# Huber loss over 8192 x 8192 floats: the middle tiles in two pieces of 6624 columns instead of three of 4416

## The chip, the core and the metric

The kernel runs on one NeuronCore of a Trainium2 chip. The metric is device time in microseconds for one execution. The parts that matter are VectorE (DVE in the profile), ScalarE (ACT), the sync engine SP, which here only issues transfers, and the core's 16 DMA engines, which move data between device memory (HBM) and the on-chip memory SBUF with its 128 partitions.

## The reference

```python
def reference(pred, target):          # both 8192 x 8192 float32
    delta = 1.0
    diff = pred - target
    abs_diff = np.abs(diff)
    return np.where(abs_diff <= delta, 0.5 * diff**2, delta * (abs_diff - 0.5 * delta))
```

The output is a float32 array of the same shape. Two arrays of 268.4 MB are read and one is written. There is no reduction: each element is computed alone.

## The kernel before

The kernel uses that the loss equals max(|d| - 0.5, 0.5 clip(d)^2), with d = pred - target and the clip to [-1, 1]. Five instructions make it, in place in two buffers a and b: VectorE subtracts (a = a - b, L82) and clips (b = clip(a), L83); ScalarE squares with a scale (b = 0.5 b^2, L86) and takes the absolute value (a = |a|, L87); VectorE closes with b = max(a - 0.5, b) (L76). b is then stored.

The arrays are seen as flat: 524288 columns for each of 128 partitions. They are cut into n = 40 tiles. Tile 0 and tile 39 are 10432 columns wide; the 38 between them have W = 13248, which is 6624 KB for one array. There are two buffers for a and two for b. Tile i uses buffer i modulo 2, and the output of a tile is stored from its b buffer.

All transfers are issued from SP's queue, in program order: the loads of tiles 0 and 1, and then for each tile i the store of tile i and the loads of tile i + 2. Each instruction of this queue waits for what it needs, and whatever is behind it waits too. The store (L68) waits for the last max of tile i. The load of a for tile i + 2 (L49) goes into the buffer that tile i has just finished with, and follows at once. The load of b for tile i + 2 must wait until the store of tile i has landed, since it overwrites what is being stored.

Middle tiles are loaded in one transfer for a and one for b. Tiles 0 and 1 arrive in halves (`HALVES`, L51). Tile 38 arrives as three quarters of a, half of b, the last quarter of a, the other half of b; tile 39 in six pieces (L55 and L56). The last tile is also stored in pieces: three of two eighths, two of one eighth.

`compute(i)` (L70) cuts a tile into pieces of equal width: 2 for tile 0, 4 for tile 38, 8 for tile 39 (`PARTS`, L58), and 3 for all others (L80), which makes pieces of 4416 columns. For each piece it issues subtract and clip on VectorE and Square and Abs on ScalarE. The max of a piece is not issued at once, since it needs ScalarE's result: pieces wait in the list `todo`, and `finish(keep)` (L73) issues the max of the oldest until only `keep` are left. With `finish(2)` (L89) VectorE is up to two pieces ahead of ScalarE; in a tile of three pieces all subtracts and clips come first, then the three maxes. The order is written out by hand: no scheduler moves anything.

Of the kernel before, what the change touches and what calls it, by code (L numbers as in the profile page):

```python
# [1 line left out]

# [4 lines left out]


@with_exitstack
def kernel(  # L10
    ctx: ExitStack,
    tc: tile.TileContext,
    pred: bass.AP,
    target: bass.AP,
    out: bass.AP,
):
    nc = tc.nc
    P = 128
    fp32 = mybir.dt.float32
    Alu = mybir.AluOpType  # L20
    Act = mybir.ActivationFunctionType
    SQRT_HALF = 0.70710678118654752

    total = pred.shape[0] * pred.shape[1] // P
    W = 13248

    ends = total % W + W
    widths = [ends - ends // 2] + [W] * (total // W - 1) + [ends // 2]
    n = len(widths)
    starts = [sum(widths[:i]) * P for i in range(n)]  # L30

    def block(x, i):
        flat = x.rearrange("r m -> (r m)")
        return flat[starts[i] : starts[i] + P * widths[i]].rearrange("(p m) -> p m", p=P)

    pool = ctx.enter_context(tc.tile_pool(name="slots", bufs=1))
    a_slots = [pool.tile([P, W], fp32, name=f"a{k}") for k in range(2)]
    b_slots = [pool.tile([P, W], fp32, name=f"b{k}") for k in range(2)]

    def shares(i, parts):  # L40
        w = widths[i] // parts
        edges = [k * w for k in range(parts)] + [widths[i]]
        return [slice(edges[k], edges[k + 1]) for k in range(parts)]

    def load(i, which, first, last):
        quarters = shares(i, 4)
        c = slice(quarters[first].start, quarters[last].stop)
        dst, src = (a_slots, pred) if which == "a" else (b_slots, target)
        nc.sync.dma_start(out=dst[i % 2][:, c], in_=block(src, i)[:, c])  # L49

    HALVES = (("a", 0, 1), ("b", 0, 1), ("a", 2, 3), ("b", 2, 3))  # L51
    LOADS = {
        0: HALVES,
        1: HALVES,
        n - 2: (("a", 0, 2), ("b", 0, 1), ("a", 3, 3), ("b", 2, 3)),  # L55
        n - 1: (("a", 0, 2), ("b", 0, 0), ("b", 1, 1), ("b", 2, 2), ("a", 3, 3), ("b", 3, 3)),  # L56
    }
    PARTS = {0: 2, n - 2: 4, n - 1: 8}  # L58

    def store(i):  # L60
        if i == n - 1:
            eighths = shares(i, 8)
            pieces = [slice(eighths[k].start, eighths[k + 1].stop) for k in (0, 2, 4)]
            pieces += eighths[6:]
        else:
            pieces = shares(i, 1)
        for c in pieces:
            nc.sync.dma_start(out=block(out, i)[:, c], in_=b_slots[i % 2][:, c])  # L68

    def compute(i):  # L70
        todo = []

        def finish(keep):  # L73
            while len(todo) > keep:
                a, b = todo.pop(0)
                nc.vector.scalar_tensor_tensor(  # L76
                    out=b, in0=a, scalar=-0.5, in1=b, op0=Alu.add, op1=Alu.max
                )

        for c in shares(i, PARTS.get(i, 3)):  # L80
            a, b = a_slots[i % 2][:, c], b_slots[i % 2][:, c]
            nc.vector.tensor_tensor(out=a, in0=a, in1=b, op=Alu.subtract)  # L82
            nc.vector.tensor_scalar(  # L83
                out=b, in0=a, scalar1=-1.0, scalar2=1.0, op0=Alu.max, op1=Alu.min
            )
            nc.scalar.activation(out=b, in_=b, func=Act.Square, scale=SQRT_HALF)  # L86
            nc.scalar.activation(out=a, in_=a, func=Act.Abs)  # L87
            todo.append((a, b))
            finish(2)  # L89
        finish(0)  # L90

    ctx.enter_context(tc.manual_schedule())

    def load_all(i):
        for piece in LOADS.get(i, (("a", 0, 3), ("b", 0, 3))):
            load(i, *piece)

    load_all(0)
    load_all(1)
    for i in range(n):  # L100
        compute(i)
        store(i)
        if i + 2 < n:
            load_all(i + 2)


# [1 line left out]
_INS = ['pred', 'target']  # L108
_OUTS = [((8192, 8192), 'float32')]


# [23 lines left out]
```

## Time and profile before

| what | value |
|---|---|
| median of 3 runs | 1868.83 us (1868.62 to 1869.63) |
| the profiled execution | 1869.48 us |
| its span, first to last instruction | 1867.7 us |
| VectorE busy | 1405.9 us, 375 instructions |
| ScalarE busy | 903.7 us, 251 instructions |
| read and written | 536.87 MB and 268.44 MB, 431 GB/s over the span |
| VectorE's wait for loads of b | 442.1 us in 41 waits |
| ScalarE's wait for the clip | 949.7 us in 48 waits |
| SP's wait for stores to land | 994.6 us in 38 waits |

The span is what the profiler sees between the first and the last instruction. The page lists busy time by engine, a strip of 40 equal slices of the span with the busy share of each engine and of the DMA engines in tenths, the DMA queues, the chain of work that ended last, the costliest groups of instructions, and the DMA issues with the median time from issue to landing. A group's line reads: source line, engine, operation, output and inputs by tile name, shape, count, busy time in us, mean duration of one in ns, and then the idle time of the engine just before these instructions and what ended it. SPq is SP's queue.

### The profile page before, as it was taken

What the parts mean: (1) busy time and instruction counts of PE and PEld (TensorE: products, weight loads), DVE (VectorE), ACT (ScalarE), POOL (GpSimd) and SP (SyncE); (2) the same over time, 40 slices, a digit from 0 to 9 for tenths busy, and PEclk for the clock granted to TensorE, in tenths of its full rate; (3) what the DMA queues carried; (4) which work ended last, traced back from release to release, by engine and by line L of the source; (5) the groups of instructions that cost most, each with busy time, mean ns of one, the idle gap of its engine ahead of it and who ended that gap; (6) DMA issues with size and microseconds to landing.
All of it is one profiled execution on the core that took longest, in us unless ns stands there. A gap on an engine that the chain in (4) does not pass through costs nothing.

```text
span 1867.7 us, 983 instructions
## 1 busy us (share of the span) xinstructions
DVE 1405.9 (75%) x375; ACT 903.7 (48%) x251; POOL 0.2 (0%) x4
## 2 busy tenths in 40 slices
DVE  4877777777777777777777777777777777777796
ACT  4444444444444444444444444444444444444464
POOL 0000000000000000000000000000000000000000
DMA  9999999999999999999999999999999999999998
GB/s 410 432 429 434 432 436 433 435 433 431 431 436 431 436 434 436 435 431 431 434 434 435 435 435 436 435 429 434 434 431 436 434 435 436 435 429 435 430 428 377
DMA packets 19303, 805.37 MB, mean 431 GB/s; under 512 B 2144, under 2 KB 2144, under 8 KB 2400
## 3 DMA queue, kind: packets, MB, share of 16 engines
q1 hardware_dynamic: 19296, 805.31, 99.8%
q14 instruction: 7, 0.06, 0.0%
HBM read 536.87 MB, written 268.44 MB: 431 GB/s over the span
## 4 chain that ended last, share of the span: by engine, by line
DMA 60%; DVE 38%; issue 1%; ACT 0%; DVEq 0%; another core or an unknown queue 0%; SPq 0%
DMA b<-in_target_dram 32%; DMA out_dram<-b 28%; DVE a L82 15%; DVE b L76 15%; DVE b L83 8%; ACT b L86 0%; ACT a L87 0%; DVEq L130 0%; SPq L49 0%; DVEq L82 0%
## 5 line engine op out<-in xcount | busy, mean ns | idle before, releaser
L86 ACT ACTIVATE b<-b 128x4416 f32<-128x4416 f32 (+3 forms) x125 | 461.0, 3688 | 949.7 <-DVE b L83 949.7
L82 DVE TENSOR_TENSOR a<-a,b 128x4416 f32<-128x4416 f32 (+3 forms) x125 | 565.2, 4522 | 442.1 <-DMA b<-in_target_dram 442.1
L76 DVE SCALAR_TENSOR_TENSOR b<-a,b 128x4416 f32<-128x4416 f32 (+3 forms) x125 | 558.5, 4519 | 3.6 <-ACT a L87 3.6
L87 ACT ACTIVATE a<-a 128x4416 f32<-128x4416 f32 (+3 forms) x125 | 460.3, 3682 | 0.0
L83 DVE TENSOR_SCALAR b<-a 128x4416 f32<-128x4416 f32 (+3 forms) x125 | 293.0, 2344 | 4.3
L86 ACT ACT_TABLE_LOAD x1 | 1.3, 1283 | 0.7 <-PEq L119 0.7
L119 POOL MEMSET const-bfloat16-1.0<- 128x1 bf16 x1 | 0.1, 101 | 0.0
L119 POOL MEMSET const-uint8-127<- 128x1 uint8 x1 | 0.1, 101 | 0.0
L119 POOL MEMSET const-float32-0.0<- 128x1 f32 x1 | 0.1, 98 | 0.2 <-issue 0.2
L119 POOL MEMSET const-float32-1.0<- 128x1 f32 x1 | 0.1, 98 | 0.0
## 6 DMA issues: line engine op xcount, KB each, us to landing
out_dram<-b SPq DMA_DIRECT2D x38, 6624.0 KB, 26.9
a<-in_pred_dram SPq DMA_DIRECT2D x36, 6624.0 KB, 42.1
b<-in_target_dram SPq DMA_DIRECT2D x36, 6624.0 KB, 31.3
b<-in_target_dram SPq DMA_DIRECT2D x4, 3312.0 KB, 35.5
a<-in_pred_dram SPq DMA_DIRECT2D x2, 3312.0 KB, 40.5
a<-in_pred_dram SPq DMA_DIRECT2D x2, 2608.0 KB, 14.5
b<-in_target_dram SPq DMA_DIRECT2D x2, 2608.0 KB, 20.3
out_dram<-b SPq DMA_DIRECT2D x1, 5216.0 KB, 21.3
```

The costliest lines, as they stand in the source:

```text
L76: nc.vector.scalar_tensor_tensor(out=b, in0=a, scalar=-0.5, in1=b, op0=Alu.add, op1=Alu.max)
L82: nc.vector.tensor_tensor(out=a, in0=a, in1=b, op=Alu.subtract)
L83: nc.vector.tensor_scalar(out=b, in0=a, scalar1=-1.0, scalar2=1.0, op0=Alu.max, op1=Alu.min)
L86: nc.scalar.activation(out=b, in_=b, func=Act.Square, scale=SQRT_HALF)
L87: nc.scalar.activation(out=a, in_=a, func=Act.Abs)
L119: nc = _bacc.Bacc("TRN2", target_bir_lowering=False, num_devices=1)
```

## The change

Every tile without an entry in `PARTS` (tiles 1 to 37) is computed in two pieces of 6624 columns instead of three of 4416. The argument of `finish` inside the loop goes from 2 to 1, so that a max is held back by one piece only. This second edit applies to every tile: in tiles 38 and 39, whose pieces stay as they were, the max of piece k now follows the clip of piece k + 1 instead of that of piece k + 2. In tile 0, with two pieces, the order of instructions stays. Loads, stores, buffers and the order of SP's queue are not touched.

```diff
-        for c in shares(i, PARTS.get(i, 3)):
+        for c in shares(i, PARTS.get(i, 2)):
             a, b = a_slots[i % 2][:, c], b_slots[i % 2][:, c]
             nc.vector.tensor_tensor(out=a, in0=a, in1=b, op=Alu.subtract)
             nc.vector.tensor_scalar(
...
             nc.scalar.activation(out=b, in_=b, func=Act.Square, scale=SQRT_HALF)
             nc.scalar.activation(out=a, in_=a, func=Act.Abs)
             todo.append((a, b))
-            finish(2)
+            finish(1)
         finish(0)
```

## The prediction

> **What bounds the kernel now.** I read the page first: engines, the DMA strip, the queues, the chain.
>
> ```profile
> DVE 1405.9 (75%) x375; ACT 903.7 (48%) x251; POOL 0.2 (0%) x4
> ...
> DMA  9999999999999999999999999999999999999998
> ...
> q1 hardware_dynamic: 19296, 805.31, 99.8%
> ...
> DMA 60%; DVE 38%; issue 1%; ACT 0%; DVEq 0%; another core or an unknown queue 0%; SPq 0%
> ```
>
> Two views disagree. The strip and the queue say that the 16 DMA engines are never idle: then only bytes count, and they do not change. The chain says that 38% of the end time is DVE, so longer work on a tile would lengthen the run. What settles it is the order of one ordinary tile. From the timeline (start, duration; SPq lines are issues, idle time in brackets):
>
> ```profile
> 999.41 4.76 DVE L82 TENSOR_TENSOR a<-a,b 128x4416 f32<-128x4416 f32 x1 [11.41 <-DMA b<-in_target_dram]
> ...
> 1014.97 0.33 SPq L49 DMA_DIRECT2D b<-in_target_dram  x1
> ...
> 1020.90 14.09 DVE L76 SCALAR_TENSOR_TENSOR b<-a,b 128x4416 f32<-128x4416 f32 x3
> ...
> 1035.02 0.34 SPq L68 DMA_DIRECT2D out_dram<-b  x1
> 1035.45 0.38 SPq L49 DMA_DIRECT2D a<-in_pred_dram  x1
> 1046.34 4.76 DVE L82 TENSOR_TENSOR a<-a,b 128x4416 f32<-128x4416 f32 x1 [11.35 <-DMA b<-in_target_dram]
> ...
> 1061.89 0.33 SPq L49 DMA_DIRECT2D b<-in_target_dram  x1
> ```
>
> A tile takes 1046.34 - 999.41 = 46.93 us. Its compute takes 1035.02 - 999.41 = 35.61; then DVE idles 11.35 until the next b lands. The list of DMA issues gives the medians from issue to landing:
>
> ```profile
> out_dram<-b SPq DMA_DIRECT2D x38, 6624.0 KB, 26.9
> a<-in_pred_dram SPq DMA_DIRECT2D x36, 6624.0 KB, 42.1
> b<-in_target_dram SPq DMA_DIRECT2D x36, 6624.0 KB, 31.3
> ```
>
> One such transfer is 6.78 MB, at the strip's 434 GB/s 15.63 us; three are 46.9, exactly the period. Assume that the queue serves transfers in single file. The store issued at 1035.02 finds a b load that ends at 1046.25; it lands 15.63 later, at 1061.88, which is 26.86 after issue. The a load issued at 1035.45 lands at 1077.51: 42.06. The b load issued at 1061.89 lands at 1093.14: 31.25. All three rows agree, so the "DMA" steps of the chain are mostly time spent in line. The slack is the 11.3 us by which a store is issued before the file reaches it. The next b load is issued when the store lands, with one a load (15.6 us) still in front of it.
>
> **The change part by part.** Prices for a 128x6624 piece come from the groups kept apart by shape, extended along the line through 4416 and 5216 columns:
>
> ```profile
> L82 DVE TENSOR_TENSOR a<-a,b 128x4416 f32<-128x4416 f32 x111 | 527.6, 4753 | 418.9 <-DMA b<-in_target_dram 418.9
> L76 DVE SCALAR_TENSOR_TENSOR b<-a,b 128x4416 f32<-128x4416 f32 x111 | 521.2, 4750 | 0.0
> L86 ACT ACTIVATE b<-b 128x4416 f32<-128x4416 f32 x111 | 429.8, 3872 | 893.5 <-DVE b L83 893.5
> L87 ACT ACTIVATE a<-a 128x4416 f32<-128x4416 f32 x111 | 429.2, 3867 | 0.0
> L83 DVE TENSOR_SCALAR b<-a 128x4416 f32<-128x4416 f32 x111 | 273.0, 2459 | 3.8
> ...
> L82 DVE TENSOR_TENSOR a<-a,b 128x5216 f32<-128x5216 f32 x2 | 11.2, 5592 | 19.7 <-DMA b<-in_target_dram 19.7
> L76 DVE SCALAR_TENSOR_TENSOR b<-a,b 128x5216 f32<-128x5216 f32 x2 | 11.2, 5589 | 3.6 <-ACT a L87 3.6
> L86 ACT ACTIVATE b<-b 128x5216 f32<-128x5216 f32 x2 | 9.1, 4550 | 25.8 <-DVE b L83 25.8
> L87 ACT ACTIVATE a<-a 128x5216 f32<-128x5216 f32 x2 | 9.1, 4533 | 0.0
> L83 DVE TENSOR_SCALAR b<-a 128x5216 f32<-128x5216 f32 x2 | 5.8, 2876 | 0.1
> ```
>
> Subtract: slope (5592 - 4753)/800 = 1.049 ns a column, so 4753 + 2208 x 1.049 = 7.07 us. Likewise the final max 7.07, clip 3.61, Square 5.74, Abs 5.71. The 1304-column subtract (1.51) lies on nearly the same line.
>
> Removed: in each of the 37 tiles of three pieces (1 to 37), three DVE and two ACT instructions. DVE work per tile goes from 3 x (4.75 + 2.46 + 4.75) = 35.89 to 2 x 17.75 = 35.49: 0.40 less. All of this is beside the transfers.
>
> Added: waits of DVE for ACT. With seams from the timeline (+0.03 or +0.04 at a dependency, -0.08 where instructions overlap), from the tile's start: subtract 0, clip 7.10, subtract 10.63, clip 17.73, free at 21.26. ACT: Square 10.75, Abs 16.41, second Square 22.03, second Abs 27.69 to 33.40. First max at 22.16 (a wait of 0.9), DVE free at 29.14; second max at 33.44 (a wait of 4.3), end 40.51. So store(i) and the a load behind it on SP's queue are issued 40.53 after the start instead of 35.61: **4.92 us later in every middle tile**. Behind the waiting max stand the tile's end and the next tile's subtract, whose data come 6.4 later (46.93 - 40.53). Store and a load still join the file 6.4 us before it runs out: cost 0. If that cover were gone, each microsecond over it would be paid in every tile.
>
> Tile 1 (arriving in halves) ends about 91.8 by the same sum from its start at 51.29, instead of 88.81; the b load then on its way lands at 104.3. Cost 0. Tile 0 keeps its order.
>
> Tile 38: store(37) goes out at 1751.01 + 40.53 = 1791.5, not 1786.6; the file then holds loads until 1797.9. Tile 38 starts 4.9 later; its first and second max come one piece earlier, its last waits 2.5 us for ACT. The same bookkeeping (3.60, 1.89, 2.96, 2.95, 3.60) gives 38.9 instead of 36.5: store(38) at 1830.35, not 1823.01. Store(37) lands at 1813.57 whatever DVE does; tile 39's loads are 9.2 + 5 x 3.08 = 24.6 us of file, to 1838.2. Cover 7.9; cost 0.
>
> Tile 39 keeps eight pieces, but `finish(1)` makes the max of piece k-1 follow the clip of piece k. With 1.51, 0.84, 1.29, 1.27, 1.51 its compute takes 31.6 against 29.9, and ends at 1861.95, not 1855.92. The file needs the five stores at 1853.8, 1856.9, 1860.0, 1863.0 and 1864.6; they are issued at 1840.5, 1848.0, 1855.4, 1859.2 and 1861.95. The last has 2.65 us. What a transfer costs beside its bytes on an empty queue is in the first load: issue 0.73, first subtract 15.86, less 2 x 6.15 us of bytes, leaves 2.8 for start and receipt. 1861.95 + 2.8 + 1.54 = 1866.3; the last store now lands about 10.7 after its issue at 1855.94, at 1866.6. I take 0. Bounds: no gain is possible, since the file is full before it; at most 2.5 lost, were that 2.8 nearly doubled.
>
> Instruction fetches: queue 14 moved 7 packets. One lies in the stretch 846 to 893, where a store took 27.66 instead of 26.87 to land; another store took 27.67 (issued 1504.26). So two of seven hit the latest engine, 0.8 each. With 185 of 983 instructions gone some 1.3 fetches go too: 1.3 x 1.6/7 = -0.3, bounds -1.6 and +0.8.
>
> Sum: 1869.48 - 0.3 = 1869.2 for the profiled execution, whose span is 1867.7 with 1.8 around it. The median of the runs stands 0.65 lower, so **1868.5**.
>
> **Rivals.**
>
> *The chain is right (slower).* If the loop b load, compute, store, b load is the bound, 4.92 is paid in each of the 19 tiles the chain passes (1, 3 to 37): +93, about 1962. For it: 38% DVE on the chain. Against it: the three landing times above. It decides once compute takes over 46.9 less a store's start (at most 2.8), so from some 44 us; I expect 40.5. [...]
>
> *Engines out of step (slower).* In the last microseconds DMA's share falls slowly (0.92 in 1860 to 1861, then 0.50, 0.31, 0.28, 0.10, 0.06), so the 16 engines end some 5 us apart and the foremost could run dry before a store issued 6.4 ahead starts. Alone that costs nothing, as the last engine sets each landing. But starting together may be dear: two tiles on the chain first took 95.17 (from 151.82), then 94.38 and 94.15, and later 93.85. Were the first value kept for 18 pairs: 18 x 1.32, less the 2.15 already paid, is +21.6, about 1890. Against it: the steady period holds with store issues 11 us ahead, and a spread once made remains.
>
> *Fewer instructions count (faster).* If DVE's work were in series, 37 x 0.40 = 14.8 would go: about 1854. DVE's 11.35 idle in every tile speaks against it. [...]
>
> **How the numbers follow.** Within 0.2% (3.7 us, about what a measurement here can tell) is the forecast, 0.86. The chain 0.03, engines out of step 0.06, a tail dearer than its bound 0.02: slower 0.11. Fewer instructions 0.03: faster. The range is the forecast's: 1868.5 - 1.6 and the runs' spread below it give 1866.5; 1868.83 + 2.5 + 0.8 and some spread give 1872.4. The rivals lie outside, 0.12 in all.
>
> **What would show it.** Right: 74 subtracts of 128x6624 at 7.07; starts 46.9 apart; DVE's wait for b down from 11.35 to about 6.4; a new wait of the max for Abs of about 5.2 a tile; stores landing 21.9 after issue, a loads 37.1, b loads still 31.3; queue 1 near 99.8%. Wrong: a tile period over 47, a b load landing sooner after its issue than 31, or gaps in the DMA strip before the last slice.

## The result

The changed kernel is **slower**: 1881.62 us median (1880.99 to 1883.68, 6 runs) against 1869.15 (1868.26 to 1869.63, 6 runs) for the kernel before. The ratio is 1.007, with a 95% interval of 1.0059 to 1.008: 12.5 us, where no change was forecast. The profiled execution took 1881.18 us with a span of 1879.1.

The page of the changed kernel shows the puzzle at once (queue and chain of the kernel before are shown in the prediction). These are its span, its first queue and its chain:

```profile
span 1879.1 us, 794 instructions
...
q1 hardware_dynamic: 19296, 805.31, 99.8%
...
DMA 54%; ACT 24%; DVE 21%; issue 1%; SPq 0%; ACTq 0%; DVEq 0%
```

The same 19296 packets with the same bytes take the same 99.8% of a span that is 11.4 us longer. So the DMA engines did not stand idle for the lost time: their packets took longer. Summed over the 16 engines, 0.998 x 16 x 11.4 is some 180 us more for the same bytes.

The compute of a tile came out as forecast. From the groups of the changed kernel, kept apart by shape:

```profile
L76 DVE SCALAR_TENSOR_TENSOR b<-a,b 128x6624 f32<-128x6624 f32 x74 | 522.3, 7058 | 183.5 <-ACT a L87 183.5
L82 DVE TENSOR_TENSOR a<-a,b 128x6624 f32<-128x6624 f32 x74 | 522.0, 7054 | 256.2 <-DMA b<-in_target_dram 256.2
...
L83 DVE TENSOR_SCALAR b<-a 128x6624 f32<-128x6624 f32 x74 | 267.1, 3610 | 2.6
```

Durations of 7.06, 7.05 and 3.61 us are what the line through the shorter pieces gave, and the new wait of the max for Abs is 183.5/37 = 4.96 us a tile (5.2 forecast). The timeline of two tiles in the middle of the run shows what follows:

```profile
995.54 0.34 SPq L68 DMA_DIRECT2D out_dram<-b  x1
...
1003.33 7.06 DVE L82 TENSOR_TENSOR a<-a,b 128x6624 f32<-128x6624 f32 x1 [7.82 <-DMA b<-in_target_dram]
...
1025.43 7.06 DVE L76 SCALAR_TENSOR_TENSOR b<-a,b 128x6624 f32<-128x6624 f32 x1 [0.79 <-ACT a L87]
...
1036.66 7.06 DVE L76 SCALAR_TENSOR_TENSOR b<-a,b 128x6624 f32<-128x6624 f32 x1 [4.17 <-ACT a L87]
1043.74 0.34 SPq L68 DMA_DIRECT2D out_dram<-b  x1
...
1050.22 7.06 DVE L82 TENSOR_TENSOR a<-a,b 128x6624 f32<-128x6624 f32 x1 [6.50 <-DMA b<-in_target_dram]
```

Compute takes 1043.74 - 1003.33 = 40.41 us, 4.8 more than before; DVE still waits for data in every tile. But that wait alternates: 6.50 us before one tile, 7.82 before the next. Where the extra 1.3 come from stands in the chain. First the kernel before, then the changed one (start, duration, what), same stretch:

```profile
968.04 31.27 DMA b<-in_target_dram
...
1035.02 26.86 DMA out_dram<-b
...
1061.89 31.28 DMA b<-in_target_dram
...
1128.87 26.86 DMA out_dram<-b
```

```profile
970.77 32.46 DMA b<-in_target_dram
...
1043.74 22.05 DMA out_dram<-b
...
1065.81 32.09 DMA b<-in_target_dram
...
1138.41 22.12 DMA out_dram<-b
```

A step of two tiles, store to store, is 1128.87 - 1035.02 = 93.85 us before and 1138.41 - 1043.74 = 94.67 after. The stores land 4.8 sooner after their issue, as they should, being issued that much later. The b load does not keep its 31.27: it takes about one microsecond more, although its place in line, behind one a load, is the same. So a transfer in the middle of a full queue has become slower, once in two tiles. Thirteen such steps lie between the stores at 475.96 and 1707.55, together 1231.6 us; before, the same thirteen took 1692.76 - 471.13 = 1221.6. That is 10.0 of the 11.4 us. The bandwidth by stretch shows when it begins. Columns are the stretch, its length, busy time of DVE, ACT and POOL, clock, DMA share and GB/s; the kernel before, then the changed one:

```profile
100.00:500.00 400.00, 301.28 (x77) 192.28 (x51) 0.00 (x0) 1.00 1.00 432
500.00:1100.00 600.00, 450.37 (x115) 285.47 (x76) 0.00 (x0) 1.00 1.00 434
1100.00:1700.00 600.00, 454.44 (x116) 295.74 (x78) 0.00 (x0) 1.00 1.00 434
```

```profile
100.00:500.00 400.00, 300.41 (x51) 187.33 (x34) 0.00 (x0) 1.00 1.00 432
500.00:1100.00 600.00, 444.18 (x77) 286.50 (x51) 0.00 (x0) 1.00 1.00 431
1100.00:1700.00 600.00, 450.64 (x77) 292.88 (x52) 0.00 (x0) 1.00 1.00 430
```

Up to 500 us the two are alike. Then the kernel before speeds up to 434 GB/s and the changed one falls to 431 and 430, at a DMA share of 1.00 in all six.

### The profile page after: what moved, and what is told of

Its sections match the earlier page's. It is cut to its first block, busy times and chain, and to the rows that moved or that the text cites. A ratio compares the mean times of both kernels' runs of the same rounds, so it can differ in the third digit from the quotient of the medians.

```text
span 1879.1 us, 794 instructions
## 1 busy us (share of the span) xinstructions
DVE 1401.9 (75%) x264; ACT 896.9 (48%) x177; POOL 0.2 (0%) x4
## 3 DMA queue, kind: packets, MB, share of 16 engines
q1 hardware_dynamic: 19296, 805.31, 99.8%
## 4 chain that ended last, share of the span: by engine, by line
DMA 54%; ACT 24%; DVE 21%; issue 1%; SPq 0%; ACTq 0%; DVEq 0%
DMA b<-in_target_dram 32%; DMA out_dram<-b 22%; ACT a L87 12%; ACT b L86 12%; DVE a L82 9%; DVE b L76 8%; DVE b L83 4%; SPq L49 0%; ACTq L130 0%; DVEq L82 0%; DVEq L83 0%
## 5 line engine op out<-in xcount | busy, mean ns | idle before, releaser
L86 ACT ACTIVATE b<-b 128x6624 f32<-128x6624 f32 (+3 forms) x88 | 454.1, 5161 | 973.0 <-DVE b L83 973.0
L82 DVE TENSOR_TENSOR a<-a,b 128x6624 f32<-128x6624 f32 (+3 forms) x88 | 559.7, 6360 | 276.0 <-DMA b<-in_target_dram 276.0
L76 DVE SCALAR_TENSOR_TENSOR b<-a,b 128x6624 f32<-128x6624 f32 (+3 forms) x88 | 560.0, 6364 | 191.2 <-ACT a L87 191.2
L87 ACT ACTIVATE a<-a 128x6624 f32<-128x6624 f32 (+3 forms) x88 | 453.3, 5152 | 0.0
L83 DVE TENSOR_SCALAR b<-a 128x6624 f32<-128x6624 f32 (+3 forms) x88 | 287.1, 3263 | 3.0
## 6 DMA issues: line engine op xcount, KB each, us to landing
a<-in_pred_dram SPq DMA_DIRECT2D x36, 6624.0 KB, 37.4
```

What stands on the lines that cost most here:

```text
L76: nc.vector.scalar_tensor_tensor(out=b, in0=a, scalar=-0.5, in1=b, op0=Alu.add, op1=Alu.max)
L83: nc.vector.tensor_scalar(out=b, in0=a, scalar1=-1.0, scalar2=1.0, op0=Alu.max, op1=Alu.min)
```

## The theories

**A, cover.** Each transfer leaves 16 receipts in the trace, which I take as one from each DMA engine. First and last receipt of a transfer lie 0.6 us apart at the start of the run, 3.5 at 500 us, and up to 5.5 later in the kernel before. I read this as 16 lines, one for each engine, in which an engine that was held up stays behind. The store must therefore be there not 0, but some 5.5 us before the *last* engine needs it, plus about 1.1 us to start (the first load is issued at 0.73, the first packets begin at 1.73 to 1.97) and 0.5 for the receipt (last packet of the run to 1866.3, receipt at 1866.8). That is about 7.1 us. The changed kernel has 6.4. By this theory its foremost engines run dry, wait for the store and start it together, and packets get slow when engines change transfers together. This is the prediction's second rival.

**B, piece size.** Instructions of 6624 columns disturb the transfers. **C, the tail.** `finish(1)` in tiles 38 and 39 costs the time. **D, plain delay.** Each microsecond by which a store is late costs its share, without a threshold (the chain read literally would be an extreme of this).

## The experiments

### Delay alone, in three doses

The kernel before, with part of the last max of tiles 1 to 37 done a second time. The maximum with the same value changes nothing in the output; the store and the a load behind it become late.

```diff
         finish(0)
+        if 0 < i < n - 2:
+            for cols in (4416,):          # (2208,) and (4416, 2208) in the other two
+                again = slice(W - cols, W)
+                todo.append((a_slots[i % 2][:, again], b_slots[i % 2][:, again]))
+            finish(0)
```

> Kernel before, three pieces of 4416, but in tiles 1 to 37 the last max is done a second time on the same 4416 columns (it changes nothing in the result), so store(i) and the a load behind it are issued some 4.7 us later, as in the changed kernel. Theory A, cover: what costs is only that the store joins the queue 6.4 us instead of 11.3 us ahead, less than the foremost DMA engine is ahead of the last one plus the start of a store; engines that ran dry then start together and packets at the change of transfers get slower. Then this is slow like the changed kernel: 1879 to 1884 us, with queue 1 still near 99.8%. Theory B, piece size: 6624-column instructions disturb the transfers: then about 1869. Theory C, the tail: tiles 38 and 39 with finish(1) cost the 12 us: then about 1869.

Measured: 1879.16 us (1876.67 to 1881.92), ratio 1.0057 (1.0042 to 1.0072). A kernel without any 6624-column instruction and with the old tail loses 10.5 us: B and C fall as explanations of the bulk. Nor is it VectorE's work as such: VectorE is busy for 1582.0 us here, but the changed kernel loses as much with 1401.9, less than the 1405.9 of the kernel before. Its profile has the mark of the changed kernel, a slow b load in every step of two tiles:

```profile
1519.22 22.11 DMA out_dram<-b
...
1541.35 32.25 DMA b<-in_target_dram
...
1614.09 22.08 DMA out_dram<-b
...
1636.19 32.33 DMA b<-in_target_dram
```

> As the run with 4416 columns done again, but 2208: stores 2.4 us later than in the kernel before, so some 9 us ahead of the queue's end. Theory A says there is a threshold: engines some 5.5 us apart and about 1.1 us of start and 0.5 us of receipt need 7.1 us, so 9 us is enough and the time stays at 1868 to 1871. If each microsecond of delay costs its share instead (no threshold), half of the 12 us: about 1875. Theories B and C: about 1869.

Measured: 1869.78 us (1869.02 to 1871.0), ratio 1.0007 (0.9998 to 1.0017). Half the delay costs 1.1 us by the medians and at most 3.2 by the interval, not 5 to 6. Its chain is that of the kernel before, with the store landing 24.36 us after issue and nothing else changed:

```profile
1506.82 24.36 DMA out_dram<-b
...
1531.21 31.26 DMA b<-in_target_dram
...
1600.67 24.34 DMA out_dram<-b
...
1625.02 31.29 DMA b<-in_target_dram
```

24.34 less 15.63 for its own bytes is 8.7 us of cover, above the 7.1. D, from zero on, does not hold.

> As above, with 4416 and then 2208 columns done again: stores 7.1 us later, some 4.2 us ahead of the queue's end. Theory A: engines are held within about 2.5 us of each other and start together in every tile, not in every second one: 37 times some 1 us, so about 1900, at least 1885. If cost goes by the delay alone: 12.5 x 7.1/4.9, about 1887. Theories B and C: about 1869.

Measured: 1885.4 us (1884.57 to 1885.93), ratio 1.0089 (1.0074 to 1.0104). Slower, as A says, but far from the 1900 that I worked out from it, and about at what D gives. In its bandwidth by stretch the loss begins earlier:

```profile
100.00:500.00 400.00, 357.35 (x93) 190.57 (x51) 0.00 (x0) 1.00 1.00 430
500.00:1100.00 600.00, 539.25 (x139) 287.17 (x76) 0.00 (x0) 1.00 1.00 428
1100.00:1700.00 600.00, 541.21 (x140) 294.68 (x78) 0.00 (x0) 1.00 1.00 429
```

So the price of a tile was mis-sized: the loss is not 1 us a tile but about that of the changed kernel, some 1 us in two tiles, only from 300 us on instead of from 500.

### Cover given back

The changed kernel, with the stores of tiles 1 to 37 in two halves; the first can go out once the first max is done.

```diff
         else:
-            pieces = shares(i, 1)
+            pieces = shares(i, 2 if 0 < i < n - 2 else 1)
```

> The changed kernel with its two pieces of 6624 and finish(1), but the store of tiles 1 to 37 in two halves, the first issued as soon as the first max is done (about 29.2 us after the tile's start, 17 us ahead of the queue's end), the second when the second max is done at 40.5, with 7.8 us of bytes in front of it. Theory A: no engine runs dry any more, so the loss goes and the time is 1868 to 1872. Theory B: computing is the same as in the changed kernel, so about 1881. Theory C: about 1881.

Measured: 1871.36 us (1871.04 to 1872.36), ratio 1.0015 (1.0005 to 1.0024). With the computing of the changed kernel, waits for ACT included, ten of the 12.5 us are gone. The loads of a land as late as in the changed kernel (37.4 us after issue at the median in both), so their lateness alone does not cost. The halves also move in packets of 26496 bytes where the whole store had 52992; this run alone can't tell an earlier store from smaller packets, but the three doses above changed the time with packets as before. The bandwidth does not fall in the course of the run:

```profile
100.00:500.00 400.00, 300.01 (x51) 186.91 (x34) 0.00 (x0) 1.00 1.00 432
500.00:1100.00 600.00, 447.78 (x77) 286.93 (x51) 0.00 (x0) 1.00 1.00 432
1100.00:1700.00 600.00, 454.57 (x78) 293.32 (x52) 0.00 (x0) 1.00 1.00 433
```

For the 2.7 us left over, the same edit to the kernel before:

> The kernel before, three pieces of 4416 and finish(2), with the stores of tiles 1 to 37 in two halves, both issued about 30 to 36 us after the tile's start. It prices the split by itself: 37 more transfers. Theory A says that the changed kernel with split stores was cured of its whole loss and that the 2.7 us left there are the price of the split, each half landing 7.9 us after the one before it instead of 7.8: then this run has the same 2 to 3 us over the kernel before, 1870.5 to 1872. If the split costs nothing, 1868 to 1869.5, and part of the changed kernel's loss stayed uncured.

Measured: 1872.33 us (1871.71 to 1872.81), against 1869.27 for the kernel before on the same chip; ratio 1.0017 (1.0007 to 1.0026). So about 3.1 us (1.3 to 4.9 by the interval) are the price of 37 more transfers, as much as the 2.7 left over, and no loss of the changed kernel that could be measured remains when its stores go out early. This also means that the split, though it cures the changed kernel, does not beat the kernel before.

### The two edits apart

First the changed kernel with `finish(2)`, which touches tiles 38 and 39 alone:

```diff
-            finish(1)
+            finish(2)
```

> The changed kernel with finish(2) again: tiles 1 to 37 are as in the changed kernel (with two pieces both maxes come last either way), tiles 38 and 39 as in the kernel before. Theory A (cover of the store in the middle tiles): still slow, 1880 to 1883 us. Theory C (the tail's new order of maxes): back to about 1869.

Measured: 1881.44 us (1880.17 to 1884.18), ratio 1.0065 (1.0048 to 1.0082). The whole loss is there without the new tail. C falls altogether; with the new tail the time is 1881.62, so the tail costs nothing that can be measured, as predicted.

Then the kernel before with `finish(1)`, where a tile of three pieces has its first max between the second and the third subtract:

```diff
-            finish(2)
+            finish(1)
```

> The kernel before with finish(1) alone: three pieces of 4416, the first max between the second and the third subtract. The third Abs then ends about 34.6 us after the tile's start and the last max about 39.4, so the store is issued 3.8 us later than before, 7.5 us ahead of the queue's end. Theory A: engines may then be about 5.8 us apart before one runs dry; the spread gets there late in the run if at all, so a small loss, 1869 to 1873 us. If cost went by the delay alone from zero on: 12.5 x 3.8/4.9, about 1879. Theory C: about 1881.

Measured: median 1869.43 us, but the ten runs fall in two groups: six from 1868.0 to 1869.73, four from 1876.74 to 1879.48. The ratio over all is 1.002 (1.0004 to 1.0036) and describes neither group. Stores land 23.1 us after issue, so the cover is 7.5, next to the 7.1 of theory A. The one execution that left a trace is of the quick group; its engines came to 5.4 us apart and no further, which by theory A asks for 7.0 of cover. One step more of the 0.8 that an instruction fetch can add (last section) would ask for 7.8. That a run tips over when its engines happen to spread a little more fits, but there is no trace of a long run to show it.

### Where in the run the delay counts

The 4416-column delay again, in tiles 1 to 12 alone, and in tiles 13 to 37 alone.

```diff
-        if 0 < i < n - 2:
+        if 0 < i < 13:                    # 12 < i < n - 2 in the other
```

> The run with 4416 columns done again, but in tiles 1 to 12 alone. Theory A: early in the run the engines are still within 4 us of each other, so a store 6.6 us ahead of the queue's end is early enough and nothing is lost: 1868 to 1870.5 us. If each delayed tile costs its share, 12 of 37 times 10.5 us: about 1872.

Measured: 1870.21 us (1868.92 to 1872.33), ratio 1.001 (1.0 to 1.0019).

> The run with 4416 columns done again, but in tiles 13 to 37 alone. Theory A: the engines are 4 us apart and more by then, so nearly the whole loss stays: 1876 to 1881 us. If each delayed tile costs its share, 25 of 37 times 10.5 us: about 1876.

Measured: 1877.51 us (1871.37 to 1881.35, 5 runs), ratio 1.0043 (1.0023 to 1.0064). The early twelve cost 1.8 us and the late twenty-five 9.1, together about the 10.5 of all. Theory A expected up to 2 and some 8 to 13, a plain share 3.4 and 7.1. The medians are on the side of A, but the late one's five runs are wide enough apart to hold both (three from 1877.51 to 1881.35, two at 1872.6 and 1871.37); taken alone these two decide little. The profiles decide more. The early one keeps the bandwidth of the kernel before throughout, also where every tile was delayed; the late one falls to that of the changed kernel. First the early one, then the late one, whose profile is of its longest run:

```profile
100.00:500.00 400.00, 339.19 (x85) 192.07 (x51) 0.00 (x0) 1.00 1.00 432
500.00:1100.00 600.00, 464.04 (x118) 285.67 (x76) 0.00 (x0) 1.00 1.00 434
```

```profile
500.00:1100.00 600.00, 494.37 (x124) 285.82 (x76) 0.00 (x0) 1.00 1.00 431
1100.00:1700.00 600.00, 513.19 (x129) 295.75 (x78) 0.00 (x0) 1.00 1.00 429
```

### What the packets show

Worked out from the trace's records of DMA packets and receipts. Cover is the median time from a store's issue to its landing less 15.6. Spread is the time from a transfer's first receipt to its last, and the next column the time from its first receipt to its tenth, at the median: how close together the ten foremost engines are. A packet of 52992 bytes takes 1.956 us at the median; one that takes over 10% more is counted as slow. Engine idle time is what is missing to 16 data packets of the queue in flight. Cover and the times are for the whole run, the rest for 1000 to 1700 us, some 5700 packets.

| kernel | cover, us | spread, us | ten foremost within, us | slow packets | engine idle time, us per 100 us | median, us |
|---|---|---|---|---|---|---|
| before | 11.3 | 4.4 to 5.5 | 0.71 | 3 | 0.35 | 1869.15 |
| delay 2208 | 8.8 | 3.4 to 4.6 | 0.87 | 2 | 0.35 | 1869.78 |
| `finish(1)` alone | 7.5 | 4.4 to 5.4 | 1.70 | 12 | 0.41 | 1869.43 (this one 1869.73) |
| delay 4416 | 6.8 | 4.3 to 5.6 | 0.43 | 193 | 1.06 | 1879.16 |
| changed kernel | 6.7 | 4.3 to 5.6 | 0.43 | 193 | 1.22 | 1881.62 |
| delay 6624 | 4.8 | 2.1 to 3.3 | 0.30 | 253 | 1.15 | 1885.4 |

On the chips of these runs the kernel before had medians of 1868.37 to 1869.27. Idle time is tiny: 1.2 us per 100, summed over 16 engines. But its place tells: in these 700 us, within 2 us of a store's issue, the engines idle for 2.1, 2.7 and 1.8 us in all in the last three rows, and for 0.01 at most in the first three. So engines do run dry there. A further 3.5 to 4.2 us lie 16 to 18 us after the issue, at the end of the store, against 0.5 at most in the first three; what they wait for is not shown. The spread by itself doesn't tell the kernels apart, 4.4 to 5.5 before and 4.3 to 5.6 in the changed one; the ten foremost engines do, within 0.43 us of each other or less where time is lost and 0.71 or more where it isn't. With a cover of 4.8 the spread stays at 2.1 to 3.3, about what 4.8 less 1.1 and 0.5 leaves.

Slow packets are what is new, and they make up the loss: over the thirteen steps from 475.96 to 1707.55 the changed kernel has 285 of them, together 149.8 us over 1.956 each, or 9.4 for each of 16 engines, of the 10.0 us lost; the kernel before has 6 in its thirteen steps, 2.2 us. The run with the changed kernel's computing and split stores has 3 from 1000 to 1700 us. They come in bunches, 138 of the 193 from 14 to 18 us after a store's issue, when engines that took up the store at once would be at the end of it. In the changed kernel, of the store issued at 948.65, ten engines begin their last packet within 0.35 us (963.23 to 963.56), and these packets take 2.07 to 3.03 us instead of 1.96. At 995.96 to 1000.16 a second bunch of seven, 2.4 to 3.1 us each, falls on the b load that the engines behind still have to finish, while the ones ahead have gone on; that transfer's last receipt comes 16.86 us after that of the one before, not 15.64. In the kernel before, no packet between 940 and 1011 us takes over 1.98 us. The spread shows the cycle: in the changed kernel it stands at 4.4 after a store that came too late, grows by the 1.2 of the slow b load to 5.6, is 5.2 to 5.3 for the next three transfers, and is cut back to 4.4 two tiles later. The store between has a microsecond more cover (7.8 in place of 6.5), because the slow b load in front of it ends later; that fits a loss in every second tile only.

## Why the prediction was wrong

**The step that failed** is "Store and a load still join the file 6.4 us before it runs out: cost 0". The 6.4 was right: DVE's wait in the rows above is 6.50 where the stores are too late. What was wrong is the queue that it was held against. The single file, which gave all three landing times, describes the *last* of 16 engines, since a landing is the last receipt. The foremost are up to 5.5 us ahead, and 6.4 is less than 5.5 + 1.1 + 0.5. In place of 0 the late stores cost 12.5 us, about 1 in a step of two tiles.

**The spread was seen and set aside.** The second rival named all the parts: engines some 5 us apart, the foremost running dry, starting together being dear. It got 0.06, on the ground that the steady period held with stores 11 us ahead "and a spread once made remains". Both are true of the kernel before and say nothing of one with 6.4. Its place was right, and its mechanism is the one that fits; its price was mis-sized: not 1.32 us over 18 steps less 2.15 (+21.6), but 0.8 to 1.2 in eleven of the thirteen steps after 475.96 (10.0 net of what these steps cost before), since, as the traces suggest, the spread has to grow first.

**The other rivals** fell as expected. The loop of the chain is not the bound: 4.8 us in 19 tiles would have been some 90 us, and DVE still waits 276 us in all for b. Fewer instructions gained nothing: with 794 instead of 983 the span is 11.4 us longer. The DMA strip of the changed kernel is full, yet its DMA engines do wait, so briefly (1.22 us per 100, summed over 16 engines) that the strip's 9s, and the 99.8%, don't show it: the late store did cost, through dearer packets.

**The rest held.** Prices of the pieces to 0.03 us; compute of a tile 40.41 for 40.53; tile 1 and the tail at no cost; stores landing 22.05 where the cover was short (21.9 forecast), a loads 37.4 at the median (37.1). "b loads still 31.3" was the line that failed, and it was named as one to look at. The instruction queue moved 6 packets instead of 7, near the 5.7 of the estimate, and one fetch fewer is lost in a change of 12.5 us.

**What stays open.** That packets slow down when engines change transfers together is read from where the slow packets lie, and from the first 500 us, when the engines are still close together and all kernels run at 430 to 433 GB/s: 31 packets of the kernel before are slow there, against 3 from 1000 to 1700 us, most of them in bunches 47 us apart, 7 to 13 us after a store's issue, where the foremost engines change to it. It was not produced by itself, and what inside the DMA path makes them slow is not known. Shown by runs: the loss follows the store's cover, has a threshold between 8.8 and 6.8 us, needs neither the larger pieces nor the new tail, and goes when the store is early.

## What to carry over

In this case slack before the queue runs dry had to be measured to the foremost engine, not to the last: take the time by which a transfer is issued ahead of its turn, and subtract how far the engines stand apart (the slow fall of the DMA share at the end of the run shows it: in the kernel before from 0.92 in 1860 to 1861 us to 0.06 in 1865 to 1866) and the start of a transfer (some 1.1 us). The DMA queue's 99.8% stood beside 431 GB/s over the span before and 429 after, so it doesn't tell whether transfers run at their best; compare GB/s at equal share, stretch by stretch (434 and 430 from 1100 to 1700 us, both at 1.00). A kernel that sat just at this threshold (7.5 us of cover) took the short time in six runs and the long one in four, so a change that eats cover "for free" should leave a margin.

## What was not expected of the hardware

The 16 engines drift apart, in the kernel before from 0.6 us at the start to 5.5 at the end of the run, and there they do not come together again before the end. After the first 500 us the spread grows in two larger steps, both at instruction fetches (two of five in that time): it goes from 3.7 to 4.5 at the landing at 874.18 and from 4.6 to 5.4 at the one at 1485.00, each time 11 us after a packet of the instruction queue (863.15 and 1473.97). These are the two fetches that the prediction priced at 0.8 each. `finish(1)` alone has the same step behind its fetch at 1473.9. If theory A holds, such a step also raises the cover that a store needs. Being apart seems to help: with the ten foremost engines 0.71 us apart, 3 packets of 5730 were slow, with them within 0.43 us, 193 and more. By the split stores of the kernel before, a transfer in two halves cost about 3.1/37 = 0.08 us more than one whole; its packets are then 26496 bytes instead of 52992, so this may be the price of more packets as much as of one more transfer.
